# The opening of a decoder layer: four column tiles of the first feed-forward block, one after the other or side by side

## The chip, the cores and the metric

The kernel runs on one core of one Trainium2 chip. The metric is the device time of one execution in microseconds (us); before the change the median of three runs is 1243.37 us (1241.1 to 1243.56). About 0.2% (2.5 us) is what a measurement of this kernel can tell from no change.

## What is computed

One decoder layer on 512 tokens of width 1024, in float32: a SwiGLU feed-forward block (width 2816), two token mixers side by side, attention into a memory of 256 tokens, and a second SwiGLU block, each with a residual sum and a layer norm.

```
def swiglu(x, w1, w3, w2):
    return (jax.nn.silu(x @ w1) * (x @ w3)) @ w2
...
    h = x
    for l in range(DEPTH):
        h = layer_norm(ALPHA * h + 0.5 * swiglu(h, ffn1_w1[l], ffn1_w3[l], ffn1_w2[l]),
                       ln1_g[l], ln1_b[l])
        mix = parallel_mixer(h, ...)
        h = layer_norm(ALPHA * h + mix, ln2_g[l], ln2_b[l])
        h = layer_norm(ALPHA * h + memory_attention(h, mem, ...), ln3_g[l], ln3_b[l])
        h = layer_norm(ALPHA * h + 0.5 * swiglu(h, ffn2_w1[l], ffn2_w3[l], ffn2_w2[l]),
                       ln4_g[l], ln4_b[l])
```

The change touches only the opening of the first block: x times the first two column tiles (128 columns each) of w1 and of w3.

## The kernel before, in words

Every float32 operand is split into two parts, `hi` (a cast to the matmul's type) and `lo` (what the cast lost); `split` (line 252) issues both. The cast goes to ScalarE or VectorE, whichever the planner thinks sooner free, the difference always to VectorE. A product is three matmuls (`mm3`, line 262): hi by hi, hi by lo, lo by hi. The first operand of `mm3` is a 128x128 block of the weights, the second 512 tokens of the transposed activations, `hT`.

The order on each engine is made by a planner. `Issue` (line 63) holds vector, scalar and load operations back with an estimated cost (`form`, line 162) and a due time, and lets each go when its engine is estimated to be free; matmuls go out as the generators reach them. Weights are fetched ahead in the order of a plan (`Weights`, line 274, at most five at a time), and their splits get 4 us of slack (`LATER`). A scheduling framework below then allots buffers and semaphores, and moves loads that wait for nothing ahead. Each load issued from SyncE gets one of eight semaphores in turn, and a load that gets one still in use waits for the earlier load on it to land.

`first_loads` (line 342) opens the program: it loads the first weight tile (w1, 128x1024, in three pieces) and the eight 128-row contraction tiles of x, alternately and all from SyncE, and splits them. `W.fill()` then fetches the three other tiles (512 KB each, rows of 4 KB) and the blocks of the first "unit". `up` (line 660) computes the four tiles pw1_0, pw3_0, pw1_1, pw3_1 one after the other, each over all eight contraction tiles (`project`, line 363): 24 matmuls of 512 columns a tile, 96 in all.

Meanwhile `sums_of_h` (line 540) makes sums and differences of quarters of x, the S tiles. The rest of the first product runs over units of two column tiles with seven products instead of eight (`products`, line 569): px (form 1), pz (5), px (6), pz (3), px (7), py (2), px (4), 24 matmuls of 256 columns each. `Unit.make` (line 516) makes each form's weights from four blocks: VectorE adds, a cast, a VectorE difference (wp_hl in the rows). Five buffers hold split weights, those of the first four tiles among them.

## Time and profile before

| | |
|---|---|
| median of three runs | 1243.37 us |
| the profiled execution | 1243.1 us, span 1241.3 us |
| TensorE (PE) busy | 1216.4 us, 98% |
| VectorE (DVE) busy | 996.3 us, 80% |
| ScalarE (ACT) busy | 533.5 us, 43% |
| HBM read and written | 149.72 and 42.60 MB |

The profile is of one execution: the span is from its first to its last instruction. All times in the views count from the span's start. Matmuls overlap in the pipeline, so the time from one start to the next, not the length shown, is what one costs.

### The profile page before, as it was taken

How to read it: one execution, taken by the hardware profiler on the slowest of the kernel's cores; microseconds unless marked ns; L12 is line 12 of the kernel's file. 1: busy time of each engine (PE TensorE's matmuls, PEld its weight loads, DVE VectorE, ACT ScalarE, POOL GpSimd, SP SyncE). 2: the span in 40 equal slices, each digit the busy share in tenths (PEclk: the TensorE clock that was granted, in tenths of full speed). 3: DMA queues.
4: the chain of work that ended last, by engine and by line, in shares of the span. 5: the costliest groups of instructions: out<-in, count | busy, mean ns of one | idle time of the engine just before them, and what ended most of it. 6: DMA issues, size and time to landing. Idle time of an engine off the chain costs nothing.

```text
span 1241.3 us, 19337 instructions
## 1 busy us (share of the span) xinstructions
PE 1216.4 (98%) x7554; PEld 1083.7 (87%) x7554; DVE 996.3 (80%) x1565; ACT 533.5 (43%) x953; POOL 111.3 (9%) x105
## 2 busy tenths in 40 slices
PE   8999999999999999999999999999999999999997
PEld 6989898989899787877778888888899898999996
DVE  8999989898853899666666694554899998999986
ACT  5344636362243476334441244442543445444421
POOL 0001121112001000000000000000010102130210
PEclk9999999999999899999999999999999999999999
DMA  9649495968634312232233445234593667795972
GB/s 348 206 113 294 95 254 132 267 136 154 221 126 101 95 57 73 62 104 85 86 102 102 168 155 186 68 119 153 191 301 87 193 181 187 188 229 145 193 178 104
DMA packets 86111, 193.57 MB, mean 156 GB/s; under 512 B 7907, under 2 KB 9699, under 8 KB 86020
## 3 DMA queue, kind: packets, MB, share of 16 engines
q1 hardware_dynamic: 66436, 154.59, 37.7%
q0 software_dynamic: 19584, 37.75, 17.5%
q8 instruction: 59, 0.97, 0.3%
q14 instruction: 32, 0.26, 0.1%
HBM read 149.72 MB, written 42.60 MB: 155 GB/s over the span
## 4 chain that ended last, share of the span: by engine, by line
PE 87%; DVE 8%; ACT 2%; issue 1%; DMA 1%; SPq 0%; POOL 0%; DVEq 0%; POOLq 0%; ACTq 0%
PE pxwp L260 18%; PE pzwp L260 9%; PE dx L260 7%; PE pywp L260 4%; PE mq L260 4%; PE res_w_o L260 4%; PE res_w L260 3%; PE pgd L260 3%; PE res_mem_w_o L260 3%; PE dz L260 3%; PE pw L260 2%; PE mk L260 2%; PE vd L260 2%; PE pw_gm L260 2%; PE qd L260 2%; PE kd L260 2%
## 5 line engine op out<-in xcount | busy, mean ns | idle before, releaser
L178 DVE TENSOR_TENSOR wp_hl<-wp_b,wp_hl 128x1024 fp32r<-128x1024 f32 x140 | 168.3, 1220 | 13.4 <-ACT wp_hl L178 8.6
L260 PE MATMUL pzwp<-S,wp_hl 128*128 128x256 f32 x960 | 122.1, 283 | 0.3 <-DVE S L178 0.3
L260 PE MATMUL pxwp<-S,wp_hl 128*128 128x256 f32 x960 | 122.3, 283 | 0.0
L260 PE MATMUL pxwp<-hT,wp_hl 128*128 128x256 f32 x960 | 120.3, 281 | 1.3 <-ACT wp_hl L178 1.3
L260 PEld LDWEIGHTS pxwp<-hT,wp_hl 128*128 128x128 f32 x960 | 117.6, 188 | 4.6 <-ACT wp_hl L178 1.7
L260 PEld LDWEIGHTS pzwp<-S,wp_hl 128*128 128x128 f32 x960 | 118.0, 191 | 0.5 <-DVE S L178 0.5
L260 PEld LDWEIGHTS pxwp<-S,wp_hl 128*128 128x128 f32 x960 | 118.3, 191 | 0.2 <-ACT p_wp L178 0.2
L170 POOL DMA_DIRECT2D acc<-st x56 | 69.5, 1561 | 425.8 <-ACT st L178 229.1
L178 ACT CAST wp_hl<-wp_b 128x1024 fp32r<-128x1024 f32 x69 | 72.1, 1052 | 78.4 <-PE pxwp L260 42.2
L178 DVE TENSOR_TENSOR wp_b<-wp_b,wp_b 128x1024 f32<-128x1024 f32 x80 | 97.4, 1219 | 0.5
L260 PE MATMUL dx<-wd_hl,A 128*128 128x512 f32 x384 | 93.1, 390 | 0.4 <-DVE old L178 0.4
L260 PEld LDWEIGHTS dx<-wd_hl,A 128*128 128x128 f32 x384 | 70.7, 188 | 14.8 <-issue 1.1
L178 DVE TENSOR_TENSOR wd_hl<-wd_b,wd_hl 128x1024 fp32r<-128x1024 f32 x56 | 68.4, 1221 | 9.0 <-ACT wd_hl L178 8.9
L178 ACT CAST wd_hl<-wd_b 128x1024 fp32r<-128x1024 f32 x42 | 44.2, 1052 | 43.7 <-PE pxwp L260 22.2
L260 PE MATMUL pywp<-hT,wp_hl 128*128 128x256 f32 x480 | 60.7, 280 | 0.3 <-ACT wp_hl L178 0.3
L260 PEld LDWEIGHTS pywp<-hT,wp_hl 128*128 128x128 f32 x480 | 58.3, 188 | 0.5 <-ACT wp_hl L178 0.5
L178 DVE CAST wp_hl<-wp_b 128x1024 fp32r<-128x1024 f32 x71 | 50.0, 704 | 8.9 <-PE ds L260 3.9
L260 PE MATMUL pw<-hT,w_hl 128*128 128x256 f32 (+1 forms) x288 | 50.6, 337 | 6.1 <-DVE w_hl L178 4.9
L260 PEld LDWEIGHTS pw<-hT,w_hl 128*128 128x128 f32 x288 | 43.3, 197 | 12.6 <-ACT hT L178 6.5
L260 PE MATMUL pgd<-hT,w_gd_hl 128*128 128x512 f32 x192 | 47.5, 400 | 0.0
L260 PE MATMUL dz<-wd_hl,A 128*128 128x512 f32 x192 | 46.7, 390 | 0.0
L260 PE MATMUL mq<-hT,mem_wq_hl 128*128 128x512 f32 x192 | 46.1, 398 | 0.0
(338 smaller groups left out, 2345.4 us busy)
## 6 DMA issues: line engine op xcount, KB each, us to landing
wp_b<-in_ffn_w SPq DMA_DIRECT2D x160, 256.0 KB, 6.7
acc<-st POOLq DMA_DIRECT2D x56, 512.0 KB, 9.7
wd_b<-in_ffn_w SPq DMA_DIRECT2D x40, 512.0 KB, 8.9
w_raw<-in_ffn_w SPq DMA_DIRECT2D x19, 512.0 KB, 5.2
wd_b<-in_ffn_w POOLq DMA_DIRECT2D x16, 512.0 KB, 14.3
h_dram<-acc SPq DMA_DIRECT2D x12, 512.0 KB, 3.3
acc<-old SPq DMA_DIRECT2D x8, 512.0 KB, 6.6
w_gm_raw<-in_w_gate SPq DMA_DIRECT2D x8, 512.0 KB, 8.0
```

What stands on the lines that cost most here:

```text
L170: return (name, 1000.0, 4000.0, lambda: getattr(engine, op)(*args, **kw)), args[:1], list(args)
L178: return (name, ns, 1500.0 if name == "sync" else 0.0, lambda: getattr(engine, op)(*args, **kw)), outs, ins
L260: issue.pe(lambda: nc.tensor.matmul(ps, w, x, start=start, stop=stop, skip_group_check=again), ps, w, x)
```

## The change

The first four column tiles are computed together. `first_loads` now loads and splits all four weight tiles, each in three pieces (contraction tiles 0-1, 2-3 and 4-7), and issues these twelve loads from ScalarE's queue; x stays on SyncE's queue. The raw weights lie in the general pool of 20 buffers. `first` replaces `up`: for contraction tiles 0 to 5 it does one tile of all four products in turn, and then finishes the products one by one with tiles 6 and 7. The planner's table gains a cost for loads from ScalarE.

```diff
+    if op == "dma_start" and name == "scalar":
+        return (name, 50.0, 1500.0, lambda: getattr(engine, op)(*args, **kw)), outs, ins
...
     def first_loads():
 
-        w = wraw.tile([P, 1024], F32, tag="raw", name="w1_raw")
-        hl = wsplit.tile([P, 2, 1024], F32R, tag="hl", name="w1_hl")
+        names = [f"w{w}_1_{f}" for f in range(2) for w in (1, 3)]
+        raws = [slot(f"{name}_raw", F32, [P, 1024]) for name in names]
+        hls = [wsplit.tile([P, 2, 1024], F32R, tag="hl", name=f"{name}_hl") for name in names]
         xT = a["xT"].rearrange("(k p) t -> p k t", p=P)
-        for k0, k1, x0, x1 in ((0, 2, 0, 1), (2, 4, 1, 2), (4, 8, 2, 4), (8, 8, 4, 6), (8, 8, 6, 8)):
-            if k1 > k0:
-                c = slice(k0 * P, k1 * P)
-                sp.dma_start(w[:, c], a["ffn1_w1"][0][:, c])
...
+        for k0, k1 in ((0, 1), (1, 2), (2, 4), (4, 6), (6, 8)):
+            if k0 % 2 == 0:
+                h_raw.append(slot(f"xT{k0}", F32))
+            raw = h_raw[-1][:, k0 % 2:k0 % 2 + k1 - k0]
+            sp.dma_start(raw, xT[:, k0:k1])
+            if k0 in (0, 2, 4):
+                c = slice(k0 * P, (2, 4, 8)[k0 // 2] * P)
+                for i, w in enumerate(raws):
+                    act.dma_start(w[:, c], a[f"ffn1_w{1 + 2 * (i % 2)}"][i // 2][:, c])
+            for k in range(k0, k1):
+                split(hT[k // 4][:, k % 4, 0], hT[k // 4][:, k % 4, 1], raw[:, k - k0])
+                if k in (0, 2, 4):
+                    for w, hl in zip(raws, hls):
+                        split(hl[:, 0, c], hl[:, 1, c], w[:, c])
...
-        def up(fs):
...
+        def first():
+
+            keys = [f"w{w}_{n}_{f}" for f in range(2) for w in (1, 3)]
+            ws, ps = [W.take(key) for key in keys], [bank(f"p{key}") for key in keys]
+            for k in range(6):
+                for w, p in zip(ws, ps):
+                    mm3(p, hl_of(w, slice(k * P, (k + 1) * P)), hk(k), k == 0, False)
+                yield
+            for i, key in enumerate(keys):
+                for k in (6, 7):
+                    mm3(ps[i], hl_of(ws[i], slice(k * P, (k + 1) * P)), hk(k), False, k == 7)
+                W.done(key)
+                if i % 2:
+                    gated(i // 2, *ps[i - 1:i + 1])
+                yield
```

Apart from line and buffer numbers, each engine's order differs from before only in its first rows: TensorE's in the 96 matmuls, VectorE's in some 110, ScalarE's in 45, SyncE's in 31; POOL's is the same. Three places follow. In brackets stand the semaphores that a row waits for; DMAHW0 to DMAHW7 are the eight of the loads, now shared by both queues.

SyncE's queue, from the program's start, before: the eleven loads of weights and x, then the first unit's blocks (wp1_1).

```order
L178 DMA xT0_99<-in_xT 128x512
L178 DMA w1_raw_97<-in_ffn1_w1 128x512
L178 DMA xT2_100<-in_xT 128x2x512
L178 DMA xT4_101<-in_xT 128x2x512
L178 DMA xT6_102<-in_xT 128x2x512
L178 DMA w3_1_0_raw_103<-in_ffn1_w3 128x1024 [waits DMAHW0_49]
L178 DMA w1_1_1_raw_105<-in_ffn1_w1 128x1024 [waits DMAHW1_49]
L178 DMA w3_1_1_raw_107<-in_ffn1_w3 128x1024 [waits DMAHW4_49,DMAHW2_49,DVE_49]
L178 DMA wp1_1_b1_110<-in_ffn1_w1 128x512 [waits DMAHW3_49]
```

And SyncE's queue of the changed kernel, from its start:

```order
L180 DMA xT0_105<-in_xT 128x512 x2
L180 DMA xT2_106<-in_xT 128x2x512
L180 DMA ident_84<-in_ident 128x128
L180 DMA small_85<-in_small 128x22 [waits DMAHW0_49]
L180 DMA mask_88<-in_mask 128x512 [waits DMAHW1_49]
L180 DMA w2_1_16_raw_2987<-in_ffn1_w2 128x1024 [waits DMAHW3_49]
L180 DMA w2_1_17_raw_3018<-in_ffn1_w2 128x1024 [waits DMAHW6_49]
L180 DMA w2_1_18_raw_3289<-in_ffn1_w2 128x1024 [waits DMAHW1_49]
L180 DMA xT4_107<-in_xT 128x2x512 [waits DMAHW5_49]
L180 DMA xT6_108<-in_xT 128x2x512 [waits DMAHW6_49]
L180 DMA wp1_1_b1_110<-in_ffn1_w1 128x512 [waits DMAHW7_49]
```

Three constants and three weight tiles that are used hundreds of microseconds later, 1.9 MB, moved from behind the first unit's blocks to between the halves of x. The load xT4 takes the semaphore of the first piece of w1_1_1, which ScalarE issues.

ScalarE, from its fifth load of the changed kernel to its first cast of xT4:

```order
L172 DMA w3_1_0_raw_98<-in_ffn1_w3 128x256
L180 CAST hT0_89<-xT2_106 128x512 [waits DMAHW5_49]
L172 DMA w3_1_0_raw_98<-in_ffn1_w3 128x512 [waits DMAHW4_49]
L172 DMA w1_1_1_raw_99<-in_ffn1_w1 128x256
L172 DMA w1_1_1_raw_99<-in_ffn1_w1 128x256 [waits DMAHW7_49]
L172 DMA w1_1_1_raw_99<-in_ffn1_w1 128x512 [waits DMAHW0_49]
L172 DMA w3_1_1_raw_100<-in_ffn1_w3 128x256 [waits DMAHW2_49]
L180 CAST w1_1_1_hl_103<-w1_1_1_raw_99 128x256 [waits DMAHW5_49]
L172 DMA w3_1_1_raw_100<-in_ffn1_w3 128x256 [waits DMAHW3_49]
L172 DMA w3_1_1_raw_100<-in_ffn1_w3 128x512 [waits DMAHW4_49]
L180 CAST w3_1_1_hl_104<-w3_1_1_raw_100 128x256 [waits DMAHW2_49]
L180 CAST hT1_90<-xT4_107 128x512 [waits DMAHW5_49]
```

Loads and casts stand in one queue now: a cast that waits for a landing holds back the loads behind it, and a load that waits for its semaphore holds back the casts. Ahead of these rows stand four loads, the load of ScalarE's function table and three casts.

VectorE before, in the stretch before form 6 of the first unit (wp1_1_6_hl):

```order
L178 TENSOR_TENSOR wp1_1_5_hl_200<-wp1_1_b0_111,wp1_1_5_hl_200 128x1024 [waits Activation_49]
L178 TENSOR_TENSOR S1_1_119<-S1_1b_126,S1_1_119 128x2x256
L178 TENSOR_TENSOR wp1_1_b0_111<-wp1_1_b0_111,wp1_1_b3_112 128x1024 [waits DMAHW5_49,DMAHW1_49,DVE_49]
L178 TENSOR_TENSOR wp1_1_3_hl_273<-wp1_1_b3_112,wp1_1_3_hl_273 128x1024 [waits Activation_49]
L178 TENSOR_TENSOR wp1_1_b1_110<-wp1_1_b1_110,wp1_1_b3_112 128x1024
L178 TENSOR_TENSOR wp1_1_6_hl_233<-wp1_1_b0_111,wp1_1_6_hl_233 128x1024 [waits PE_49,Activation_49]
L178 SCALAR_TENSOR_TENSOR G1_0_236<-pw3_1_1_282,G1_0_236 128x512 [waits PE_49]
L178 TENSOR_TENSOR S1_0_118<-S1_1a_125,S1_0_118 128x2x256
L178 TENSOR_TENSOR S1_1_119<-S1_1c_127,S1_1_119 128x2x256
```

And VectorE in the changed kernel, up to the same operation:

```order
L180 TENSOR_TENSOR S3_1_1_121<-S1_1a_125,S3_1_1_121 128x2x256 [waits Activation_49]
L180 CAST wp1_1_5_hl_301<-wp1_1_b0_111 128x1024 [waits DVE_49,PE_49]
L180 SCALAR_TENSOR_TENSOR G1_0_311<-pw3_1_0_129,G1_0_311 128x512 [waits PE_49,Activation_49]
L180 TENSOR_TENSOR wp1_1_5_hl_301<-wp1_1_b0_111,wp1_1_5_hl_301 128x1024 [waits DVE_49]
L180 TENSOR_TENSOR wp1_1_b1_110<-wp1_1_b1_110,wp1_1_b3_112 128x1024 [waits DMAHW5_49,DMAHW1_49]
L180 TENSOR_TENSOR wp1_1_b0_111<-wp1_1_b0_111,wp1_1_b3_112 128x1024 [waits DVE_49]
L180 TENSOR_TENSOR wp1_1_3_hl_320<-wp1_1_b3_112,wp1_1_3_hl_320 128x1024 [waits Activation_49]
L180 CAST wp1_1_2_hl_372<-wp1_1_b2_113 128x1024 [waits DMAHW6_49,DMAHW2_49,PE_49]
L180 SCALAR_TENSOR_TENSOR G1_0_311<-pw3_1_1_131,G1_0_311 128x512
L180 TENSOR_TENSOR wp1_1_6_hl_310<-wp1_1_b0_111,wp1_1_6_hl_310 128x1024 [waits Activation_49]
```

All of the S work stands ahead of the unit's weights now, and form 6 comes last of both where it stood before the last S tiles. Form 5 takes over the buffer of the first tile's weights, and so waits for that tile's last matmul.

## Rows read from the trace of the kernel before

**Rows 1.** Page, part 1: busy us (share of the span) xinstructions.

```profile
PE 1216.4 (98%) x7554; PEld 1083.7 (87%) x7554; DVE 996.3 (80%) x1565; ACT 533.5 (43%) x953; POOL 111.3 (9%) x105
```

**Rows 2.** TensorE's waits, whole span: us in total, times, longest.

```profile
PE pw L260 <- DVE w_hl L178: 4.9, 1, 4.9
```

**Rows 3.** Timeline of TensorE, 0 to 45 us: start, us, what, count.

```profile
4.92 0.79 PE L260 MATMUL pw<-hT,w_hl 128*128 128x512 f32 x1 [4.92 <-DVE w_hl L178]
5.99 2.50 PE L260 MATMUL pw<-hT,w_hl 128*128 128x512 f32 x5 [0.28 <-DVE hT L178]
9.35 24.09 PE L260 MATMUL pw<-hT,w_hl 128*128 128x512 f32 x90 [0.86 <-ACT hT L178]
33.28 3.01 PE L260 MATMUL pxwp<-hT,wp_hl 128*128 128x256 f32 x24
...
39.00 3.04 PE L260 MATMUL pxwp<-S,wp_hl 128*128 128x256 f32 x24
41.88 3.04 PE L260 MATMUL pzwp<-S,wp_hl 128*128 128x256 f32 x24
```

**Rows 4.** Stretches: busy us and (count) of each engine, PEclk, DMA share, GB/s.

```profile
9.35:15.00 5.65, 5.65 (x13) 4.15 (x14) 5.65 (x11) 3.89 (x6) 0.00 (x0) 1.00 1.04 410
16.00:32.00 16.00, 16.00 (x70) 12.87 (x69) 15.46 (x20) 9.76 (x13) 0.00 (x0) 1.00 1.05 389
...
41.90:60.00 18.10, 18.10 (x154) 18.10 (x153) 18.03 (x23) 7.81 (x12) 0.34 (x1) 1.00 0.53 123
...
10.50:13.50 3.00, 3.00 (x8) 2.32 (x8) 3.00 (x7) 2.13 (x4) 0.00 (x0) 1.00 1.03 415
14.00:20.00 6.00, 6.00 (x25) 4.77 (x24) 6.00 (x8) 4.90 (x6) 0.00 (x0) 1.00 1.05 388
```

**Rows 5.** Timeline of VectorE, 0 to 75 us.

```profile
3.05 0.29 DVE L178 CAST w_hl<-w_raw 128x256 fp32r<-128x256 f32 x1 [2.18 <-DMA w_raw<-in_ffn_w]
...
31.16 1.22 DVE L178 TENSOR_TENSOR wp_b<-wp_b,wp_b 128x1024 f32<-128x1024 f32 x1
32.30 1.22 DVE L178 TENSOR_TENSOR wp_hl<-wp_b,wp_hl 128x1024 fp32r<-128x1024 f32 x1
...
34.08 0.68 DVE L178 TENSOR_TENSOR S<-S_1a,S 128x512 fp32r<-128x512 f32 x1
34.68 0.68 DVE L178 TENSOR_TENSOR S<-S_1c,S 128x512 fp32r<-128x512 f32 x1
```

**Rows 6.** VectorE's groups by form, 0 to 75 us: count, busy us, mean ns.

```profile
L178 DVE CAST hT<-xT 128x512 fp32r<-128x512 f32 x3 | 1.2, 422 | 0.2 <-DMA xT<-in_xT 0.2
L178 DVE TENSOR_TENSOR w_hl<-w_raw,w_hl 128x256 fp32r<-128x256 f32 x2 | 0.9, 426 | 0.1
...
L178 DVE CAST w_hl<-w_raw 128x256 fp32r<-128x256 f32 x2 | 0.6, 294 | 3.0 <-DMA w_raw<-in_ffn_w 3.0
```

**Rows 7.** Timelines of SyncE's queue and ScalarE, 0 to 20 us.

```profile
1.18 0.42 SPq L178 DMA_DIRECT2D xT<-in_xT  x1
1.64 0.43 SPq L178 DMA_DIRECT2D w_raw<-in_ffn_w  x1
...
0.73 1.28 ACT L178 ACT_TABLE_LOAD   x1 [0.73 <-PEq L1544]
...
8.67 0.62 ACT L178 CAST hT<-xT 128x512 fp32r<-128x512 f32 x1 [2.82 <-DMA xT<-in_xT]
```

**Rows 8.** Loads issued in 0 to 20 us: KB each, median us to landing.

```profile
wp_b<-in_ffn_w SPq DMA_DIRECT2D x12, 256.0 KB, 6.3
xT<-in_xT SPq DMA_DIRECT2D x3, 512.0 KB, 6.9
...
xT<-in_xT SPq DMA_DIRECT2D x2, 256.0 KB, 3.0
w_raw<-in_ffn_w SPq DMA_DIRECT2D x2, 128.0 KB, 2.6
```

**Rows 9.** SyncE's own waits, 0 to 20 us: us in total, times, longest.

```profile
SPq L178 <- DMA w_raw<-in_ffn_w: 3.9, 4, 1.1
```

More of the change, by code (lines that the diff above doesn't have):

```diff
@@ L342, in first_loads @@
     def first_loads():
-        w = wraw.tile([P, 1024], F32, tag="raw", name="w1_raw")
-        hl = wsplit.tile([P, 2, 1024], F32R, tag="hl", name="w1_hl")
+        names = [f"w{w}_1_{f}" for f in range(2) for w in (1, 3)]
+        raws = [slot(f"{name}_raw", F32, [P, 1024]) for name in names]
+        hls = [wsplit.tile([P, 2, 1024], F32R, tag="hl", name=f"{name}_hl") for name in names]
         xT = a["xT"].rearrange("(k p) t -> p k t", p=P)
-        for k0, k1, x0, x1 in ((0, 2, 0, 1), (2, 4, 1, 2), (4, 8, 2, 4), (8, 8, 4, 6), (8, 8, 6, 8)):
-            if k1 > k0:
-                c = slice(k0 * P, k1 * P)
-                sp.dma_start(w[:, c], a["ffn1_w1"][0][:, c])
-            if x0 % 2 == 0:
-                h_raw.append(slot(f"xT{x0}", F32))
-            raw = h_raw[-1][:, x0 % 2:x0 % 2 + x1 - x0]
-            sp.dma_start(raw, xT[:, x0:x1])
-            if k1 > k0:
-                split(hl[:, 0, c], hl[:, 1, c], w[:, c])
-            for k in range(x0, x1):
-                split(hT[k // 4][:, k % 4, 0], hT[k // 4][:, k % 4, 1], raw[:, k - x0])
-        W.specs.pop(0)
-        W.tiles["w1_1_0"] = hl
-        W.held = 1
+        for k0, k1 in ((0, 1), (1, 2), (2, 4), (4, 6), (6, 8)):
[12 more added lines that the diff above has]
+                        split(hl[:, 0, c], hl[:, 1, c], w[:, c])
+        for name, hl in zip(names, hls):
+            W.specs.pop(0)
+            W.tiles[name] = hl
+        W.held = 4
     def project(name, w, toks=slice(None), o=0):
@@ L658, in gated @@
             drop(pa, pb)
-        def up(fs):
-            for f in fs:
-                ps = []
-                for w in ("w1", "w3"):
-                    key = f"{w}_{n}_{f}"
-                    ps.append((yield from project(f"p{key}", W.take(key))))
-                    W.done(key)
-                    yield
-                gated(f, *ps)
+        def first():
[12 more added lines that the diff above has]
+                yield
         def seven(p, late=()):
@@ L813, in ffn @@
             mark = sums_of_h(n, sums)
-            yield from up(range(2))
+            yield from first()
         yield mark
```

## The prediction

> **What bounds the kernel now.** First the page's engine shares [rows 1]: TensorE is busy 98% of the span, so the end moves only where TensorE idles, runs slowly or is made to wait. Then its waits [rows 2]: the longest is 4.9 us, once, for the first split weights. The timeline shows the place [rows 3]: the first matmul starts at 4.92, gaps of 0.28 and 0.86 us follow, and from 9.35 on the matmuls run without a gap through 33.28, where the first unit starts, to form 6 of it (second pxwp row, 39.00) and form 3 (second pzwp row, 41.88). Idle in the opening: 6.1 us.
>
> Third, the pace [rows 4]. From 9.35 to 15.00 there are 13 matmuls in 5.65 us, 0.43 us each: 512 columns at 1.2 GHz. From 16 to 32 there are 70 in 16 us, 0.23 us each: the 2.4 GHz level. (The clock column reads 1.00 in both; here the counts tell more than the column.) So the clock rose near 15.1, after 5.8 us without a gap and after the broken work before it; some 18 matmuls ran at the low level and lost 0.2 us each, 3.5 us. Idle and low clock together, 9.6 us, are the most that any opening could give back.
>
> Fourth, who is next. VectorE starts at 3.05 [rows 5] and then hardly rests: 5.65 of 5.65 us, 15.46 of 16, later 18.03 of 18.10 [rows 4]. It runs only a little ahead: the difference of form 6's weights starts at 32.30 and the last S tile for form 6 at 34.68, done near 35.4, for a product that TensorE begins at 39.00: a lead of 3.7 us [rows 3, 5]. And the loads run at 388 to 415 GB/s with a DMA share of about 1.0 from 9 us on [rows 4]. Whatever TensorE gains in the opening it keeps only if VectorE, and the loads that feed it, come earlier too.
>
> **The change, part by part.**
>
> *The start.* SyncE's issues follow each other by 0.46 us [rows 7]. No row shows ScalarE issuing a load; its price lies between nothing and, say, twice SyncE's, and I take SyncE's, the same kind of instruction. Four issues from 0.74 end near 2.6; the table load (1.28 us, at 0.73 before [rows 7]) now follows them, to 3.9; the first cast ends near 4.2. With x's first piece landing 3.0 us after its issue at 0.74 [rows 8], the first matmul starts at 4.2 to 4.4 in place of 4.92: 0.6 us earlier.
>
> *The third matmul.* It needs the weights' difference, and on VectorE that now stands behind a cast of the third weight piece (256 KB, tiles 4-7), which isn't needed yet. Before the change the pieces up to 1.5 MB landed at 8.65 (the cast of xT at 8.67 waited for that [rows 7]). Now 1.7 MB in two queues are ahead or beside; the third piece, with 1.0 to 1.3 MB moved, should land at 6.5 to 7.3. So two matmuls, a hole, and steady work from 7.3 to 8.0, in place of 9.35.
>
> *TensorE from there.* The other waits fall within its pace: the later pieces of w3_1_1 are needed only after 33 matmuls. When the clock rises no row can tell; I let the rise move up with the start of the steady work, by 1.4 to 2.1 us, to 13 to 14, and keep 15.1 as the late end. By 13 to 14 some 15 of the 96 matmuls are done; 81 at 0.234 us are 19 us. The opening ends at 32 to 33 in place of 33.28: a gain of 0.3 to 1.3 us for TensorE alone. (At 15.1, with 18 to 20 done, it would end near 33.2.)
>
> *VectorE.* From its first cast (x's first piece, at 3.7 to 3.9) to the difference of form 6's weights stand, counted in its new order: 7 operations over 1024 columns with two operands, at 1.14 us from start to start; 30 over 512, at 0.60 [rows 5]; 8 differences of 256 columns (0.43 us long less the 0.09 us that neighbours overlap, 0.33); 8 casts of 512 (0.42 less 0.09); 3 casts of 256 (0.29 less 0.09) [rows 6]; 2 casts of 1024 at 0.6 and 0.2 us of small ones. 8.0 + 18.0 + 2.6 + 2.7 + 0.6 + 1.2 + 0.2 = 33.3 us. Without any wait it is done at 37.2.
>
> Its waits come from the loads. ScalarE's queue goes in order: fifth load near 6.2 to 8.3 (behind the cast of w3_1_0's first piece), then a cast that waits for xT2 (7 to 8.6), then five loads at 0.46 us, a cast of w1_1_1's first piece when it lands (11 to 13), and only then the last two loads, which land at 15 to 16.8. xT4 waits on SyncE for that same w1_1_1 piece, and 1.9 MB of constants and late weights were moved ahead of it: at 0.39 MB/us they are 4.8 us of transfer. x's first half (1.0 MB), the twelve pieces (2.0), those 1.9 and xT4 (0.5) make 5.4 MB; counted from 1.7 MB at 7.0 to 8.6, at 388 GB/s [rows 4], it lands at 16.6 to 18.2, and xT6 1.3 us later. VectorE has caught up with the loads by then; adding its operations in order, with these landings, I get waits of 2.1 to 3.8 us, and form 6's difference done at 39.3 to 41.0.
>
> *Sum.* Form 6's third matmul needs that difference; two matmuls stand before it, and it and the 21 behind it, at 0.12 us (the starts 39.00 and 41.88 hold 24 [rows 3]), bring form 3 to 42.0 to 43.6. By TensorE alone it would be at 40.6 to 41.6. VectorE decides. Before it was 41.88 [rows 3]: 0.1 to 1.8 us later; I take the middle, **0.9 us later**. Behind it each engine's order is soon the same as before, and VectorE, busy 18.03 of 18.10 us there [rows 4], can't make the shift up quickly, so I carry it to the end unchanged. The wait for the first tile's buffer (form 5) costs nothing: that tile ends 4.2 us before the opening's end, near 28, and VectorE comes to form 5 near 31.5; if it came earlier it would wait there.
>
> *Small pieces.* Twelve pieces with rows of 1 and 2 KB replace three loads with rows of 4 KB. The three loads of 4 KB rows ran at 415 GB/s, those of 2 KB at 388 [rows 4]: 1.5 MB cost 0.25 us more, inside the landings above. The Trainium skill (Perfetto Trace Analysis, DMA Optimizations) says both that small transfers carry an overhead and that splitting lets work start sooner if the DMA engines idle; from 9 us on they don't idle here, so only the first half applies to the later pieces. By it alone the sum would be 0.25 us.
>
> The profiled execution took 1243.1 us (the median is 0.3 us above it): 1243.1 + 0.9 = **1244.0 us**.
>
> **The rivals.**
>
> *The loads only come sooner* (faster). The first eight loads are issued by 2.6 us from two queues instead of by 4.5 from one: 1.9 us. If all that VectorE needs moved up by that, its waits would almost vanish (done near 37.4), and form 3 would start near 40.0, 22 matmuls behind it: 1241.2 us, with TensorE's opening over by 31.4, 1.9 us sooner too. With the clock's rise at 11 and no wait of VectorE at all it is 2.7 us at most: 1240.4. For it: SyncE waits 3.9 us for semaphores in the first 20 us [rows 9], and 1.9 us of issue are real. Against it: the transfers, not the issues, are full from 9 us on [rows 4], and the compiled order puts 1.9 MB ahead of xT4. The Trainium skill (DMA: Bandwidth & Descriptors, Issuing engines are not separate DMA queues) says that loads from several engines share the same DMA engines and save only issue time; by that the gain is these 1.9 us at most. Chance 0.2, of which 0.12 by over 0.2%.
>
> *ScalarE's queue starves VectorE* (slower). One mechanism: xT4 is issued only when w1_1_1's first piece has landed, and that was issued only after ScalarE's cast of xT2. Priced with the landings of the busy stretch, 5 us for a piece (a 256 KB load takes 6.3 [rows 8]) and 6.9 for 512 KB: cast of xT2 ends 9.2, w1_1_1's piece issued 10.2, landed 15.2, xT4 at 22.1 in place of 16.6. VectorE stands from 17 to 22, form 6 is done near 44 and form 3 starts at 46.7: 4.8 us, 1247.9 us. It decides against the forecast's class when xT4 lands after about 19. For it: the eight shared semaphores and both engines in order; SyncE waits for them already before [rows 9]. Against it: the pieces are small, and 5 us assumes a backlog that ScalarE's short queue may not have. Chance 0.3.
>
> *It doesn't do what it says.* The orders above show that the tiles are interleaved and the loads are on ScalarE; what may fail is only that the four run abreast, since TensorE's order takes them in as their weights come. That is in the forecast, with no time of its own.
>
> **How the numbers follow.** The forecast (VectorE sets form 6; 0 to 1.8 us later) has 0.5, the faster rival 0.2, the slower 0.3. A measurement can tell about 0.2%, 2.5 us, from no change: below 1240.9 or above 1245.9. Faster 0.12; slower 0.3; same 0.58. The likeliest case alone spans 1242.8 to 1245.2; with the rivals' ends, less a tenth on each side, 1241.0 to 1247.8.
>
> **What would show it.** Right: TensorE's first matmul near 4.3, the opening's end at 32 to 33, then a wait on wp_hl of about 1 to 3 us in front of or inside form 6, ended by VectorE, and form 3 starting at 42 to 43.6; xT4's casts near 17 to 18; VectorE idle 2 to 4 us between 5 and 20, for loads. Wrong: VectorE idle over 5 us in that stretch (the slower rival), no wait at form 6 (the faster one), or the 96 matmuls ending before 31, which would mean an earlier rise of the clock than I took. A shift that grows after 60 us would say that carrying it unchanged was wrong.

## The result, and the profile after

The changed kernel takes **1249.69 us**, median of 4 runs (1247.47 to 1250.85), against 1242.32 of the kernel before beside it: ratio **1.0055, 95% interval 1.0039 to 1.0071**. It is about 7 us slower, outside the predicted range (1241.0 to 1247.8) on the slow side. The profiled execution took 1250.85 us, its span is 1249.1.

TensorE's timeline of the changed kernel, 0 to 75 us (start, us, what, count, idle time before and who ended it):

```profile
4.70 1.35 PE L262 MATMUL pw<-hT,w_hl 128*128 128x512 f32 x2 [4.70 <-ACT w_hl L180]
8.15 5.10 PE L262 MATMUL pw<-hT,w_hl 128*128 128x512 f32 x13 [2.10 <-DVE w_hl L180]
16.19 22.04 PE L262 MATMUL pw<-hT,w_hl 128*128 128x512 f32 x81 [2.94 <-ACT w_hl L180]
38.07 2.98 PE L262 MATMUL pxwp<-hT,wp_hl 128*128 128x256 f32 x24
...
45.69 1.34 PE L262 MATMUL pzwp<-S,wp_hl 128*128 128x256 f32 x9 [0.31 <-ACT p_wp L180]
46.87 2.80 PE L262 MATMUL pxwp<-S,wp_hl 128*128 128x256 f32 x22
...
56.77 5.80 PE L262 MATMUL pxwp<-hT,wp_hl 128*128 128x256 f32 x48
```

Against [rows 3]: 90 matmuls ran there without a gap from 9.35; here 13 run from 8.15, TensorE then stands for 2.94 us until a cast by ScalarE, and 81 are left. The opening ends at 38.07 in place of 33.28 (+4.8). The last row, the 48 matmuls of form 1 of the next unit, serves as a mark from here on. In TensorE's timeline of the kernel before it is:

```profile
50.49 5.86 PE L260 MATMUL pxwp<-hT,wp_hl 128*128 128x256 f32 x48
```

They start at 56.77 here, +6.3. Most of the loss is made in the first 57 us.

The same stretch in windows (busy us and count of PE, PEld, DVE, ACT, POOL; PEclk; DMA share; GB/s):

```profile
12.00:14.00 2.00, 1.25 (x5) 0.64 (x4) 0.38 (x2) 0.00 (x0) 0.00 (x0) 1.00 1.04 396
14.00:16.00 2.00, 0.00 (x0) 0.00 (x0) 0.48 (x2) 0.27 (x1) 0.00 (x0) 0.89 0.72 265
16.00:18.00 2.00, 1.81 (x4) 1.45 (x5) 2.00 (x7) 0.55 (x2) 0.00 (x0) 0.50 0.53 125
...
20.00:22.00 2.00, 2.00 (x6) 1.52 (x6) 0.72 (x2) 1.14 (x2) 0.00 (x0) 0.50 1.05 406
```

Ahead of the idle time TensorE was already at the 2.4 GHz level: 5 matmuls in 1.25 us. Behind it the granted clock stands at 0.50 (the 1.2 GHz level) to about 22 us: 6 matmuls in 2 us where [rows 4] have 70 in 16. VectorE has work for 0.48 of 2 us from 14 and 0.72 of 2 from 20, where [rows 4] have it busy 15.46 of 16. The DMA engines, full from 9 us on in [rows 4], carry 125 GB/s from 16 to 18. All three engines wait, and for loads. ScalarE's timeline from 8 us says for which (ACTq rows are issues of loads; the row at 8.98, the second of the five, is from the same timeline of 9 to 9.4 us):

```profile
8.11 0.35 ACTq L172 DMA_DIRECT2D w_raw<-in_ffn_w  x1
8.51 0.62 ACT L180 CAST hT<-xT 128x512 fp32r<-128x512 f32 x1
8.53 5.35 ACTq L172 DMA_DIRECT2D w_raw<-in_ffn_w  x5
...
8.98 0.45 ACTq L172 DMA_DIRECT2D w_raw<-in_ffn_w  x1
...
15.73 0.41 ACT L180 CAST w_hl<-w_raw 128x256 fp32r<-128x256 f32 x1 [6.61 <-DMA w_raw<-in_ffn_w]
15.74 0.91 ACTq L172 DMA_DIRECT2D w_raw<-in_ffn_w  x2
...
20.52 1.14 ACT L180 CAST hT<-xT 128x512 fp32r<-128x512 f32 x2 [3.12 <-DMA xT<-in_xT]
```

The timeline of SyncE's queue shows what went ahead of xT4:

```profile
5.14 3.92 SPq L180 DMA_DIRECT2D w_raw<-in_ffn_w  x3
15.73 0.89 SPq L180 DMA_DIRECT2D xT<-in_xT  x2
```

The first of the five loads from 8.53 is the last piece of w3_1_0, the second is the first piece of w1_1_1. It goes out at 8.98, behind four casts, three of which waited for loads, and is cast at 15.73, 6.7 us later. The last two pieces go out behind that cast. SyncE's xT4 goes out at the same moment: it takes the semaphore of w1_1_1's first piece. The three loads of w2 ahead of it (1.5 MB, from 5.14) were out by 9.1. The loads of this stretch (KB each, median us to landing) took, for 128 KB, 5.7 us on ScalarE's queue where [rows 8] have 2.6:

```profile
w_raw<-in_ffn_w ACTq DMA_DIRECT2D x8, 128.0 KB, 5.7
```

VectorE's waits for loads, 0 to 60 us (total, times, longest; the second row is the wait before its first cast):

```profile
DVE w_hl L180 <- DMA w_raw<-in_ffn_w: 7.9, 5, 2.0
DVE hT L180 <- DMA xT<-in_xT: 3.2, 1, 3.2
```

Its timeline: the cast of the last piece of w3_1_1, and the difference of form 6's weights, the first of the two in the second row, which [rows 5] have at 32.30:

```profile
22.31 0.43 DVE L180 CAST w_hl<-w_raw 128x512 fp32r<-128x512 f32 x1 [1.36 <-DMA w_raw<-in_ffn_w]
...
45.33 2.35 DVE L180 TENSOR_TENSOR wp_hl<-wp_b,wp_hl 128x1024 fp32r<-128x1024 f32 x2
```

That difference ends near 46.5, and the 22 matmuls that need it start at 46.87.

### The profile page after: what moved, and what is told of

The parts are those of the page before. It is cut to its first block, busy times and chain, and to the rows that moved or that the text cites. A ratio compares the mean times of both kernels' runs of the same rounds, so it can differ in the third digit from the quotient of the medians.

```text
span 1249.1 us, 19349 instructions
## 1 busy us (share of the span) xinstructions
PE 1218.5 (98%) x7554; PEld 1083.9 (87%) x7554; DVE 997.5 (80%) x1577; ACT 530.9 (43%) x953; POOL 112.5 (9%) x105
## 4 chain that ended last, share of the span: by engine, by line
PE 79%; DVE 9%; DMA 6%; ACT 3%; issue 2%; SPq 0%; ACTq 0%; POOL 0%; POOLq 0%; DVEq 0%
PE pxwp L262 17%; PE pzwp L262 8%; PE dx L262 5%; PE pywp L262 4%; PE mq L262 4%; PE res_w_o L262 4%; PE res_w L262 3%; PE pgd L262 3%; PE res_mem_w_o L262 3%; DMA acc<-st 2%; PE mk L262 2%; PE vd L262 2%; PE qd L262 2%; PE pw_gm L262 2%; PE kd L262 2%
```

## The experiments

Ratios are against the kernel before, run beside each; "opening" is the start of the first pxwp row, "mark" that of the 48 matmuls, both from the profiled run. The mark's distance from 50.49 follows the total within some 1.2 us in all but the noisiest (f16): what is won or lost here is mostly won or lost in the first 57 us.

| kernel | median us (runs) | ratio [95%] | opening | mark |
|---|---|---|---|---|
| before | 1241.82 to 1242.89 | 1 | 33.28 | 50.49 |
| the change | 1249.69 (4) | 1.0055 [1.0039, 1.0071] | 38.07 | 56.77 |
| a2_late_weights_behind | 1246.05 (6) | 1.0037 [1.0024, 1.0051] | 35.12 | 53.98 |
| b_pieces_on_sync | 1242.75 (10) | 1.0006 [0.9993, 1.0018] | 32.83 | 50.50 |
| e2_queue_alone | 1247.78 (5) | 1.0053 [1.0033, 1.0072] | 40.09 | 57.24 |
| f16_filled_hole | 1250.42 (4) | 1.0073 [1.0046, 1.0099] | 37.98 | 56.45 |
| s1_competing_loads | 1244.21 (10) | 1.0016 [1.0005, 1.0026] | 33.84 | 51.48 |
| p2_larger_pieces | 1242.23 (12) | 1.0003 [0.9993, 1.0013] | 32.12 | 49.77 |
| k_first_pieces_on_scalar | 1240.97 (12) | 0.9988 [0.9978, 0.9998] | 30.50 | 48.32 |
| b3_casts_on_scalar | 1243.29 (12) | 1.0010 [1.0000, 1.0020] | 33.23 | 50.89 |
| l2_later_tiles_on_scalar | 1244.71 (10) | 1.0014 [1.0002, 1.0026] | 34.55 | 52.28 |
| kp_first_on_scalar_larger | 1240.24 (12) | 0.9982 [0.9971, 0.9992] | 30.53 | 48.22 |
| kc_unit_casts_on_scalar | 1241.38 (12) | 0.9990 [0.9980, 1.0001] | 32.56 | 49.69 |
| kcp_both | 1239.48 (12) | 0.9976 [0.9966, 0.9987] | 30.47 | 48.11 |

### The order on SyncE: a2_late_weights_behind

```diff
-        raws = [slot(f"{name}_raw", F32, [P, 1024]) for name in names]
+        raws = [slot(f"{names[0]}_raw", F32, [P, 1024])]
+        raws += [wraw.tile([P, 1024], F32, tag="raw", name=f"{name}_raw") for name in names[1:]]
```

> The changed kernel, but only the first of the four weight tiles has its raw pieces in the large store; the other three take theirs from the three buffers that raw weights share. So w2's three late weight tiles wait for those buffers, and SyncE's order is x's first half, x's second half (xT4, xT6), the eight 256 KB loads of the first unit's weights, and only then constants, mask and w2. ScalarE's queue and the side-by-side order stay. Theory 1 (the 1.9 MB moved ahead of xT4 on SyncE make xT4 and, by sharing the DMA engines, the pieces late): xT4's casts move from 20.5 us to under 15, VectorE's idle time between 5 and 24 us falls from about 8 us to under 4, form 3's second product starts near 43 to 45 in place of 49.5, the total is 1241 to 1245. Theory 2 (ScalarE's own queue, in order behind its casts, is late whatever SyncE carries): w1_1_1's first piece still lands after 14 us, TensorE still stands idle for over 2 us before it and the opening still ends after 36; total 1246 to 1250. Theory 3 (computing the four side by side puts too much of VectorE's work ahead of the unit): loads are early and the opening ends near 33, and still form 3 starts 1.5 us or more late; total 1244 to 1246.

Part of the loss goes: the opening ends at 35.12, the mark stands 3.5 us late in place of 6.3, and the ratio is 1.0037 in place of 1.0055, with intervals that overlap. xT4's first cast comes at 14.70 in place of 20.52. So SyncE's order is one cause. The run changes two things in it at once: the 1.9 MB are no longer ahead of xT4, and xT4 no longer takes the semaphore of a piece of w1_1_1. All five loads of x are out by 5.4 us, where xT4 went out at 15.73 (SyncE's timeline of this kernel):

```profile
0.74 4.64 SPq L180 DMA_DIRECT2D xT<-in_xT  x5
```

Which of the two counts for more isn't shown. The order isn't the only cause, and theory 2 is seen at work: ScalarE's cast of w1_1_1's first piece still waits 5.18 us, for a load that went out behind its earlier casts (ScalarE's timeline of this kernel):

```profile
8.05 3.67 ACTq L172 DMA_DIRECT2D w_raw<-in_ffn_w  x4
13.81 0.41 ACT L180 CAST w_hl<-w_raw 128x256 fp32r<-128x256 f32 x1 [5.18 <-DMA w_raw<-in_ffn_w]
```

### Side by side without ScalarE's queue: b_pieces_on_sync

```diff
-                    act.dma_start(w[:, c], a[f"ffn1_w{1 + 2 * (i % 2)}"][i // 2][:, c])
+                    sp.dma_start(w[:, c], a[f"ffn1_w{1 + 2 * (i % 2)}"][i // 2][:, c])
```

> The changed kernel with the twelve weight pieces issued from SyncE, as all loads were before; the four column tiles are still computed side by side. SyncE's order is then x's first half and the twelve pieces mixed, xT4, xT6, the unit's weights, and constants and w2 behind them. Theory 1 and theory 2 (the lateness comes from ScalarE's queue and from what is moved up beside it) both say that the pieces land in their order by about 10 to 11 us, the hole before w1_1_1 is under 1 us, the opening ends at 31 to 34, and the total comes back to 1240 to 1243. Theory 3 (the side-by-side order costs VectorE's lead): loads in order, and still form 6's weights are done after 41 and the total is 1244 to 1246. In no case should it be over 1247.

TensorE's timeline of this kernel:

```profile
10.08 22.92 PE L262 MATMUL pw<-hT,w_hl 128*128 128x512 f32 x90 [0.70 <-ACT w_hl L180]
```

The loss is gone (1.0006, interval on both sides of 1), with the four tiles still computed side by side. The whole of it comes from the queue and from what the order did around it. Theory 3 is left with half a microsecond: the opening ends 0.45 us earlier than before, and at the mark nothing is left of it.

This kernel also tells a late issue from a slow load. The issue of w1_1_1's first piece (SyncE's timeline, 5.1 to 5.4 us), its cast by ScalarE, and the landing of the 128 KB pieces (loads issued in 0 to 24 us):

```profile
5.06 0.43 SPq L180 DMA_DIRECT2D w_raw<-in_ffn_w  x1
...
10.86 0.41 ACT L180 CAST w_hl<-w_raw 128x256 fp32r<-128x256 f32 x1 [0.84 <-DMA w_raw<-in_ffn_w]
...
w_raw<-in_ffn_w SPq DMA_DIRECT2D x8, 128.0 KB, 5.6
```

On one queue, with none of w2 beside them, the small pieces take 5.6 us, as long as on ScalarE's queue in the change (5.7). Of the 4.9 us by which the change casts this piece later (15.73 against 10.86), 3.9 are its later issue (8.98 against 5.06).

### The queue without side by side: e2_queue_alone

The kernel before, with its planner told of ScalarE's loads, and:

```diff
-            sp.dma_start(raw[:, :n], src)
+            (act if key in ("w3_1_0", "w1_1_1", "w3_1_1") else sp).dma_start(raw[:, :n], src)
...
-                sp.dma_start(w[:, c], a["ffn1_w1"][0][:, c])
+                act.dma_start(w[:, c], a["ffn1_w1"][0][:, c])
```

(w3_1_1's raw tile also comes from the large store, so that its load waits for no buffer.)

> The kernel before, one column tile after the other, with the loads of these four tiles issued from ScalarE's queue (in the sizes of before) and nothing else changed in the text; SyncE's order becomes x, then the unit's eight loads. Theory 2 (ScalarE's queue by itself costs the time): slower than before by 2 to 6 us, by late w1_1_1 and w3_1_1 (1244 to 1249). Theory 1: w2 and the constants stay behind the unit here, x lands earlier, so within 1.5 us of before (1241 to 1244). Theory 3: equal to before or up to 1 us faster, since the order of the work is that of before.

1.0053: with these loads on ScalarE the kernel is as slow as the change, in theory 2's range. But neither of TensorE's two long waits is for a load that went out late. It waits 4.90 us for the difference of x's first contraction tile, the second of the four from 9.71 in VectorE's timeline. That tile's cast began at 4.70; the difference stands behind casts on VectorE that wait for the last piece of w1 and for xT2:

```profile
7.78 0.43 DVE L180 CAST w_hl<-w_raw 128x512 fp32r<-128x512 f32 x1 [1.23 <-DMA w_raw<-in_ffn_w]
...
9.25 0.43 DVE L180 CAST hT<-xT 128x512 fp32r<-128x512 f32 x1 [0.31 <-DMA xT<-in_xT]
9.71 2.50 DVE L180 TENSOR_TENSOR hT<-xT,hT 128x512 fp32r<-128x512 f32 x4
```

In the kernel before, VectorE's first difference of x starts at 5.25. TensorE then waits 2.01 us for w3_1_0, whose load went out by 2.6 us but whose cast on ScalarE (the first of the three in its timeline here) stands behind one that waits for the unit's weights:

```profile
19.03 1.04 ACT L180 CAST wp_hl<-wp_b 128x1024 fp32r<-128x1024 f32 x1 [1.28 <-DMA wp_b<-in_ffn_w]
19.98 2.94 ACT L180 CAST w_hl<-w_raw 128x1024 fp32r<-128x1024 f32 x3
```

The size is thus this order's own: the planner moved casts and differences together with the loads, and the run doesn't price the queue by itself.

### The clock: f16_filled_hole

```diff
                 for w, p in zip(ws, ps):
+                    if k == 0 and w is ws[2]:
+                        extra = bank("extra")
+                        for i in range(16):
+                            matmul(extra, ws[1][:, 0, :P], hT[0][:, 0, 0], True, True)
+                        drop(extra)
```

> The changed kernel with 16 added matmuls of 512 columns on data that is already there, into a bank that nobody reads, ahead of the first matmul of w1_1_1: TensorE has 22 matmuls in place of 15 to run before the wait for that tile, so the 2.9 us of idle time at 13.2 us should be filled. Theory 4 (the fall of the granted clock to 0.50 from 16 to 22 us follows from that idle time, and is a loss of its own of about 14 matmuls at 0.2 us, 2.8 us): the clock reads 1.00 from 16 to 22, and the opening ends near 37.3 in place of 38.1 although 16 matmuls were added; else the clock still falls and it ends near 40. Theory 1 with the loads as the cause of the end: the total stays within 1 us of the changed kernel (1248.5 to 1250.5) even if the clock stays up, because form 6's weights come from VectorE no earlier. Theory 4 as the main cause of the total: 1246.5 to 1248.

Two windows of this kernel, to be held against those of the change:

```profile
16.00:18.00 2.00, 1.37 (x6) 0.52 (x4) 1.91 (x7) 0.40 (x1) 0.00 (x0) 1.00 0.81 178
...
20.00:22.00 2.00, 2.00 (x10) 1.63 (x9) 0.68 (x3) 1.12 (x2) 0.00 (x0) 1.00 1.06 406
```

With the hole filled (0.34 and 0.29 us are left of it) the clock stays up: 10 matmuls from 20 to 22 us where the change has 6, and the opening ends at 37.98 in spite of 16 more matmuls. So the fall of the clock follows the idle time. Yet the mark is only 0.3 us earlier and the total no better (1250.42). VectorE, in a slightly different order behind the opening, ends form 6's difference near 45.1, 1.5 us earlier than in the change, and TensorE waits at form 6 for a copy by ScalarE (timelines of VectorE and of TensorE):

```profile
43.87 1.22 DVE L180 TENSOR_TENSOR wp_hl<-wp_b,wp_hl 128x1024 fp32r<-128x1024 f32 x1
...
44.84 3.20 PE L262 MATMUL pxwp<-S,wp_hl 128*128 128x256 f32 x24 [0.97 <-ACT p_wp L180]
```

The clock's loss in the opening is thus mostly hidden behind what TensorE waits for at form 6.

### Bytes on the other queue: s1_competing_loads

b_pieces_on_sync, and in the loads of later weights:

```diff
-            sp.dma_start(raw[:, :n], src)
+            (act if key in ("w2_1_16", "w2_1_17", "w2_1_18") else sp).dma_start(raw[:, :n], src)
```

> The version with all pieces on SyncE (b_pieces_on_sync), and one thing more: the three 512 KB loads of w2's late weight tiles, which nothing needs in the opening, are issued from ScalarE's queue, two before its first cast and one behind it. Every order of SyncE, VectorE, TensorE and of the casts is that of b_pieces_on_sync. Theory A (two queues share the DMA engines, so bytes on the second queue delay the needed ones on the first by their own transfer time): at 0.39 MB/us the 1.5 MB cost up to 3.9 us; the pieces of w1_1_1 land at 13 to 16 us in place of 10.5 to 12.5, the opening ends at 35 to 37 in place of 32.8, the total is 1245 to 1248. Theory B (the cost is that loads on ScalarE stand behind its casts, which wait for loads; sharing costs little): no needed load stands on ScalarE here, so the opening ends within 1 us of 32.8 and the total is 1242 to 1243.5.

TensorE's timeline of this kernel:

```profile
7.13 1.22 PE L262 MATMUL pw<-hT,w_hl 128*128 128x512 f32 x2 [7.13 <-ACT w_hl L180]
9.62 24.38 PE L262 MATMUL pw<-hT,w_hl 128*128 128x512 f32 x94 [1.26 <-DVE w_hl L180]
```

Between the two theories: sharing is real, and smaller than theory A had it. The first matmul comes at 7.13 in place of 4.37, but the opening ends only 1.0 us later, since b_pieces_on_sync spent part of that time in holes anyway. The ratio goes from 1.0006 to 1.0016, with intervals that overlap. 1.5 MB did not cost their 3.9 us of transfer.

### Loads behind casts: k_first_pieces_on_scalar and l2_later_tiles_on_scalar

Both are b_pieces_on_sync with some pieces back on ScalarE: the first pieces of w1_1_0 and w3_1_0, ahead of every cast; or all pieces of w1_1_1 and w3_1_1, which stand behind casts.

```diff
-                    sp.dma_start(w[:, c], a[f"ffn1_w{1 + 2 * (i % 2)}"][i // 2][:, c])
+                    (act if k0 == 0 and i < 2 else sp).dma_start(w[:, c], a[f"ffn1_w{1 + 2 * (i % 2)}"][i // 2][:, c])
```

The second of them has `act if i >= 2 else sp` in this place, and the raw tiles of a2_late_weights_behind.

> b_pieces_on_sync, but the first 128 KB pieces of w1_1_0 and w3_1_0 alone are issued from ScalarE's queue, before its table load; all else stays on SyncE in the order of need. Theory A and theory B agree that this is harmless: the two are needed first, and no cast stands ahead of them. It tells whether the gain of issue time that the change was to bring exists at all: two issues of 0.47 us come off SyncE, so the third to the eighth load are issued 0.9 us earlier, the hole after the first two matmuls falls from 1.7 us to about 1, and the opening ends 0.3 to 0.9 us earlier (32.0 to 32.5). The total follows only if VectorE comes earlier too: 1241 to 1243.

> Side by side as in the change, with the pieces of w1_1_0 and w3_1_0 on SyncE and only the six pieces of w1_1_1 and w3_1_1 on ScalarE, where each stands behind one to four casts; three raw tiles share the three buffers of raw weights, so w2 and the constants stay behind the unit on SyncE. Nothing that is not needed is ahead of them on SyncE but xT4 and xT6. Against k_first_pieces_on_scalar (two pieces on ScalarE, no cast ahead) only the place of these loads differs. Theory B (a load behind casts goes out late): the first piece of w1_1_1 goes out before 5 us but the later four only after 8.5 us, land at 13.5 to 16, and TensorE, which does w1_1_0 and w3_1_0 meanwhile, waits 1 to 3 us before or among the matmuls of w1_1_1; the opening ends at 33 to 35 and the total is 1242.5 to 1245.5. Theory A alone (only unneeded bytes on the other queue hurt): the opening ends by 32 and the total is 1240.5 to 1242.

TensorE's timeline in k_first_pieces_on_scalar:

```profile
4.65 26.01 PE L262 MATMUL pw<-hT,w_hl 128*128 128x512 f32 x96 [4.65 <-ACT w_hl L180]
```

ScalarE's timeline in l2_later_tiles_on_scalar:

```profile
8.29 0.34 ACTq L172 DMA_DIRECT2D w_raw<-in_ffn_w  x1
...
10.06 2.12 ACTq L172 DMA_DIRECT2D w_raw<-in_ffn_w  x3
...
16.66 0.40 ACT L180 CAST w_hl<-w_raw 128x256 fp32r<-128x256 f32 x1 [2.48 <-DMA w_raw<-in_ffn_w]
```

TensorE's timeline in l2_later_tiles_on_scalar:

```profile
9.93 6.70 PE L262 MATMUL pw<-hT,w_hl 128*128 128x512 f32 x16 [0.51 <-ACT w_hl L180]
17.11 17.60 PE L262 MATMUL pw<-hT,w_hl 128*128 128x512 f32 x74 [0.48 <-ACT w_hl L180]
```

Two pieces on ScalarE with no cast ahead: all 96 matmuls run without a gap from 4.65, the opening ends 2.8 us before that of the kernel before, and the ratio is 0.9988. That beats what was expected of it (32.0 to 32.5): with no hole, 17 matmuls ran from 10 to 14 us, so the clock was up by 10 in place of 15. This is one execution: kc below, with the same loads in the opening, had two short holes and ended it at 32.56. Six pieces behind casts: all but the first go out from 8.29 on, one is cast at 16.66 after a wait of 2.48, and the ratio is 1.0014, 3.2 us more (0.0026 of 1242). Some 2.2 of these are k's gain over b_pieces_on_sync (1.0006) and 1.0 is l2's loss against it; the intervals of both overlap that of b_pieces_on_sync. At the mark that loss is 1.8. The waits on TensorE are shorter than expected (0.51 and 0.48); most of the difference in the opening is that the 16 matmuls up to 16.6 still took 0.42 us each, the low level.

The pair differs in more than the casts ahead. The load for which l2 waits (cast at 16.66, the first piece of w3_1_1) is the first of the three from 10.06. In k it goes out at 7.38 and is cast at 11.24 (SyncE's timeline of 7.4 to 7.8 us, and ScalarE's):

```profile
7.38 0.43 SPq L180 DMA_DIRECT2D w_raw<-in_ffn_w  x1
...
11.24 0.41 ACT L180 CAST w_hl<-w_raw 128x256 fp32r<-128x256 f32 x1 [1.33 <-DMA w_raw<-in_ffn_w]
```

In l2, xT4 and xT6 went out ahead of it, in SyncE's freed place; in k they go out behind it. SyncE's timeline in l2:

```profile
7.89 1.44 SPq L180 DMA_DIRECT2D xT<-in_xT  x2
```

So the piece goes out 2.7 us later and then takes 6.6 us in place of 3.9. Theory B holds as far as the late issue goes; the longer landing comes beside what moved up on SyncE, and the two weren't tried apart.

### Sizes and casts: p2, b3, kp, kc, kcp

p2 and kp: two pieces per tile, 256 and 768 columns. b3: the opening's casts on ScalarE alone. kc: the casts of the first unit and of the sums of h on ScalarE alone. kcp: kp and kc together.

```diff
-            if k0 in (0, 2, 4):
-                c = slice(k0 * P, (2, 4, 8)[k0 // 2] * P)
+            if k0 in (0, 2):
+                c = slice(k0 * P, (2, 8)[k0 // 2] * P)
...
-        scaled(hi, src, scale)
+        if only:
+            act.copy(hi, src)
+        else:
+            scaled(hi, src, scale)
```

> b_pieces_on_sync with two pieces per weight tile (256 and 768 columns) in place of three (256, 256, 512): eight loads, no size but that changed. If the small pieces keep the DMA engines from being full (297 GB/s from 10 to 14 us there, where the kernel before had 412), the rate in that stretch rises to 360 or more, xT4's casts start near 15 in place of 16.2, and VectorE is done with form 6's weights earlier by up to 1 us; total 1240.5 to 1242.5. If the rate is set by something else, nothing moves by over 0.5 us (1242 to 1243.5). The second piece of w1_1_0 comes later, so the hole after the first two matmuls may grow by up to 1 us without a cost at the end.

> b_pieces_on_sync, with every cast of the opening (x and the four weight tiles) put on ScalarE alone instead of on whichever of ScalarE and VectorE the planner thinks free first. ScalarE is idle for more than half of the opening, and VectorE has some 11 of these casts, 4 us. If VectorE's work sets form 6 (theory 3), its difference of form 6's weights is done before 39.5 in place of 40.5, the 0.45 us that the opening gains is kept past 60 us, and the total is 1240.5 to 1242.3. If the loads set it, nothing moves by more than 0.5 us. The other way: casts in one line on ScalarE come later than in two engines, the hole before w1_1_1 opens again, and the opening ends after 33.5: 1242.5 to 1244.

> k_first_pieces_on_scalar with two pieces per tile (256 and 768 columns), as in p2_larger_pieces: four loads fewer. The rate from 10 to 14 us (318 GB/s with the small pieces) rises to about 390, xT4 lands 1 to 1.3 us earlier. TensorE's opening was gap-free already there, so the end can gain only what VectorE makes of earlier loads: 0 to 0.8 us; a hole of up to 1 us ahead of the third k-tile (its 768-column piece lands later) is possible. 1240.0 to 1242.0.

> k_first_pieces_on_scalar with the casts of the first unit's weights and of the sums of h (not those of the opening) on ScalarE alone, which is busy 3.1 of 7 us from 33 to 40 while VectorE is busy all of it. VectorE loses four casts of 0.69 us and one of 0.42 up to 46 us. If VectorE's work is what gives back 0.65 us at form 6 (the shift against the kernel before went from 2.8 us earlier in the opening to 2.1 behind form 6), the 2.8 us stay and the total is 1239.5 to 1241.0. If ScalarE's casts come later in one line than in two, form 5 or 6 waits for them and the total is 1241 to 1243.

> Both edits on k_first_pieces_on_scalar together: larger second pieces and the unit's casts on ScalarE. If each gains what it may alone, the opening ends near 30.5, form 6 is not waited for, and the total is 1239.2 to 1241.2, the fastest of all; if the limits are elsewhere it equals k_first_pieces_on_scalar within 0.5 us.

The window from 10 to 14 us in b_pieces_on_sync:

```profile
10.00:14.00 4.00, 3.92 (x10) 2.96 (x11) 4.00 (x11) 0.83 (x3) 0.00 (x0) 1.00 0.90 297
```

The same window in p2_larger_pieces:

```profile
10.00:14.00 4.00, 4.00 (x13) 3.20 (x12) 3.97 (x9) 0.86 (x3) 0.00 (x0) 1.00 1.04 400
```

**p2**: the small pieces did keep the DMA engines from being full; with larger ones the rate is 400 GB/s and the opening ends 0.7 us earlier. A load holds one of the eight semaphores until it lands, so small pieces also mean fewer bytes on their way at a time; whether that or a price of each piece held the rate down wasn't tried. The total can't be told from that of b_pieces_on_sync. **b3** gained nothing: casts in one line come later, TensorE waits 1.56 us at 10.00 for one, the opening ends at 33.23. **kc** is inconclusive in its total: its opening happened to have two short holes (0.27 and 0.66 us, the place of its loads being the same) and ended at 32.56, but from there to the mark nothing was given back (0.72 and 0.80 us earlier than before), where k lost 0.6 of its 2.8. **kp** (0.9982) came as expected and can't be told from k. **kcp** has the lowest ratio, 0.9976 with the interval below 1: 3 us faster than the kernel before and some 10 faster than the change, with the four tiles side by side as in the change. Its interval overlaps those of k and kp, and from the opening to the mark it gives back 0.4 of its 2.8 us, kp 0.5: no gain of the unit's casts on ScalarE is shown. TensorE's timeline of kcp:

```profile
10.88 19.75 PE L265 MATMUL pw<-hT,w_hl 128*128 128x512 f32 x83 [0.20 <-DVE w_hl L180]
```

## Why the prediction was wrong

The likeliest case failed, and the slower rival came, harder than it was priced.

- **The start** (4.2 to 4.4): 4.70. The four issues took 0.47 us each and the table load followed, as taken; but the piece's cast, which was to end near 4.2, waited 0.31 us for its load and began at 4.24.
- **The third matmul** (7.3 to 8.0): 8.15, with the hole in the place and for the reason given.
- **TensorE from there**: this step failed. "The other waits fall within its pace" looked at the later pieces of w3_1_1 only. The first piece of w1_1_1 is needed after 15 matmuls, near 13.2, and was cast at 15.73. A hole of 2.94 us followed, and behind it 6 us at the low level of the clock, for which the step had no term: it asked only when the clock would rise (it had risen by about 12, before the forecast 13 to 14). The opening ended at 38.07 (32 to 33 forecast).
- **VectorE, the landings**: the root of it. The step had w1_1_1's first piece landing at 11 to 13. Its issue at 8.98, behind the cast of xT2, was about where the step had it, but 128 KB took 6.7 us. I took a short landing for a short piece: the 2.6 us of [rows 8] are those of the program's first loads. The landings of the busy stretch, which the rival used, were nearer, and b_pieces_on_sync shows that they need no second queue (5.6 us). The five issues from 8.53 took 5.35 us in place of five times 0.46; the last of them went out at 13.55. The step took xT4 from the bytes ahead of it (16.6 to 18.2 forecast, cast at 20.52), but it waited for w1_1_1's piece to land, and the DMA engines stood partly idle from 14 to 18. From this follow the two last loads, VectorE's waits behind its first cast (2.1 to 3.8 forecast; 7.9, the first of the two rows above) and form 6's difference (39.3 to 41.0 forecast; 46.5). VectorE's own work was counted nearly right: 33.3 us, and 34.3 from its first cast to the end of that difference without its idle time.
- **The sum** (+0.9): +6.3 at the mark. Form 6's 22 matmuls start some 7.6 us late (46.87, against 39.00 and two matmuls of 0.12), but TensorE runs 9 of form 3 ahead of them (the row at 45.69). "Carried to the end unchanged" was nearly right: +6.3 at the mark, +7.8 between the two spans. Of the last 1.5 us, 0.7 arise at one place, form 6 of a later unit (277.11 in the kernel before, 284.53 in the change; the product ahead of it starts at 274.24 and 280.94). Why wasn't tried.
- **The slower rival**: its mechanism and its point of decision held (xT4 after about 19): xT4 went out at 15.73, when w1_1_1's first piece was there. a2_late_weights_behind takes xT4 off that semaphore, and the 1.9 MB from ahead of it, and gives back 2.8 of the 6.3 us. The rival was under-sized: 4.8 us where the mark has 6.3. It let VectorE go on as soon as xT4 was there, but w3_1_1's last piece, sent behind the same cast, came later still: VectorE stood until 22.31 and had that split to do first.
- **The faster rival**: the saving of issue time exists in part. k_first_pieces_on_scalar takes two issues off SyncE and gains 2.2 us at the mark; it ended the opening at 30.50, below the 31.4 of that rival, through the earlier clock. The Trainium skill (DMA: Bandwidth & Descriptors, Issuing engines are not separate DMA queues) says that loads of several engines run on the same DMA engines and interleave. s1_competing_loads agrees: 1.5 MB on the other queue moved the first matmul from 4.37 to 7.13. What the prediction made of that rule was only an upper bound for a gain; in s1_competing_loads the loads that aren't needed yet, with a queue of their own, ran beside those that were.
- **Small pieces** (0.25 us): "from 9 us on the DMA engines don't idle here" was read from the kernel before and didn't hold after: shares of 0.72 and 0.53 from 14 to 18 us. Between b_pieces_on_sync and p2_larger_pieces the small pieces cost 0.7 us of the opening.
- **The chances**: slower had 0.3, and the range ended 1.9 us short, since the rival's end rested on one price for a landing and on xT4 as the last load that VectorE waits for.

What stays open: how the 7 us split between SyncE's order (a2 gives back nearly half at the mark) and the loads behind casts (the rest, by b) can't be added up exactly, since each makes the other worse; whether xT4's place or its semaphore counts; and a ScalarE queue with all pieces ahead of every cast wasn't tried.

## What to carry to other kernels

Here a second engine's queue paid only for loads that are needed first and go out before that engine's first compute instruction. A load behind a cast goes out when the cast's own load has landed, and loads that wait on each other so form a chain; two loads that share a semaphore are chained too. When a load leaves a queue, look at what moves up in its place: here the order filled SyncE with 1.9 MB that nobody needed yet and pushed the second half of the input behind it. To see whether idle time on the busiest engine matters, look at which engine is late next: filling TensorE's hole gave nothing in the total, since VectorE was waiting for the same loads. And take a load's landing time from a stretch with as much on its way: 128 KB took 2.6 us at the start and 5.6 in the busy stretch, on one queue or two.

## What the runs showed of the hardware

The granted clock fell to 0.50 in a hole of 2.94 us without a matmul, and stayed up with one of 0.34 (f16). Between these it isn't certain: near 427 us TensorE is idle for 1.94 us before the products sm, in the profiles of all fourteen kernels. In twelve of them the 14 products behind it take 3.5 to 4.2 us, in kcp_both and l2_later_tiles_on_scalar 3.03. In the kernel before the clock fell behind it, in kcp_both it didn't, with the same work and the same wait. TensorE's timeline in the kernel before:

```profile
427.52 4.16 PE L260 MATMUL sm<-kT,qT 96*128 96x512 f32 x14 [1.94 <-ACT qT L178]
```

The same products in kcp_both:

```profile
425.43 3.03 PE L265 MATMUL sm<-kT,qT 96*128 96x512 f32 x14 [1.94 <-ACT qT L180]
```

The window from 430 to 440 us in the kernel before:

```profile
430.00:440.00 10.00, 10.00 (x44) 8.59 (x43) 7.68 (x31) 4.55 (x15) 0.00 (x0) 0.75 0.14 40
```

And in kcp_both:

```profile
430.00:440.00 10.00, 10.00 (x56) 8.20 (x55) 9.92 (x40) 7.34 (x24) 0.00 (x0) 1.00 0.14 40
```

The clock column reads 0.75 in the one and 1.00 in the other, and the 14 products take 4.16 and 3.03 us. Falls of the clock go with a good part of the 5.8 us by which runs of one kernel differ (1239.09 to 1244.91 for the kernel before in the last comparison): the 11 runs with a mean granted clock of 0.998 or 0.999 have a median of 1240.24, the 24 with 0.994 to 0.997 one of 1243.59. Where in these runs the clock fell isn't on record. So the time of one profiled run is no verdict: l2_later_tiles_on_scalar had no fall there and took 1242.83, while its median is 1244.71.
